# Block transposes inside the out-projection, a later last turn, and one pair of modulation columns as a row on TensorE, in a two-layer encoder

## Chip, cores and metric

One core of a Trainium2 chip. The metric is the device time of one execution in microseconds (us). An execution runs five engines side by side, each with its own stream of instructions in a fixed order: TensorE (PE, matmuls), VectorE (DVE), ScalarE (ACT), GpSimdE (POOL) and SyncE (SP, which here issues the DMA transfers). Products are accumulated in PSUM; operands lie in SBUF.

## The reference

Two layers over 1024 tokens of width 1024, each a mixer and an MLP. Layer A mixes with an mLSTM, layer B with latent attention; what is common to both is this:

```python
def rms_norm(x, g):
    xf = x.astype(jnp.float32)
    y = xf * lax.rsqrt(jnp.mean(xf * xf, axis=-1, keepdims=True) + EPS)
    return (y * g.astype(jnp.float32)).astype(x.dtype)

def modulate(h, shift, scale):
    return h * (1 + scale[:, None, :]) + shift[:, None, :]
...
    c_act = jax.nn.silu(c)
    for layer in range(DEPTH):
        sh1, sc1, g1, sh2, sc2, g2 = jnp.split(c_act @ mod_w[layer] + mod_b[layer], 6, axis=-1)
        h = modulate(rms_norm(x, norm_g[layer, 0]), sh1, sc1)
        if layer < N_A:
            y = mlstm_mixer(h, a_w_in[layer], a_b_gates[layer], a_head_norm[layer], a_w_out[layer])
        else:
            ...
            y = mla_mixer(h, b_w_qa[j], b_q_norm[j], b_w_qb[j], b_w_o[j], k_nope, k_rope, v, cos, sin)
        x = x + g1[:, None, :] * rms_norm(y, norm_g[layer, 1])
        h = modulate(rms_norm(x, norm_g[layer, 2]), sh2, sc2)
        y = sq_relu_mlp(h, ffn_w1[layer], ffn_w2[layer])
        x = x + g2[:, None, :] * rms_norm(y, norm_g[layer, 3])
    return x
```

At the end of the mLSTM mixer stands `(sigmoid(o_pre) * rms_norm(hh)) @ w_out`. All is in fp32.

## The kernel before

**Products.** An fp32 product is made of three passes of a shorter format: each operand is split into a high part (a cast on ACT, tiles `whi`, `hSh`, `hTh`, `aTh`) and a low part (a subtraction on DVE, `wlo`, `hSl`, `hTl`, `aTl`). `mm3` issues high by high (L159), low by high (L160) and high by low (L161). The tiles lie in a few rotating buffers: PSUM tiles of two banks (`mm`) and of one (`sm`). A tile that is asked for again waits until its last reader is done. The order of each engine's instructions is fixed when the program is built, from the order of the code and from a scheduler's estimate of when things are ready; `issue_after` pins the instructions in it behind a given one.

**The start.** The token blocks are normed and then modulated with per-column scale and shift. Blocks 0 to 3 come first: ACT squares them, DVE makes the reciprocal root (`rsqrt`), ACT scales them by it (L945), PE transposes them by columns k (128 of the 1024 each), and ACT applies the column's scale and shift while it reads PSUM (tile `t`, L953) and casts it. The scale and shift (`modcol`) are a product of a vector `cact` with a 1024x2048 part of `mod_w`, which arrives in `slab` tiles, two columns k to a slab, four units of 512 KB each. Column 0 is made by PE from 16 matmuls of one column (L1011). The others are summed on DVE over the rows (`mod_sum`, L998 and L1000: one TENSOR_SCALAR and seven SCALAR_TENSOR_TENSOR) and turned into a column by a matmul with ones (L1008). The first products are the value projections of blocks 0 to 3, one group for each k.

**The mLSTM's end.** `mlstm_chunk` is a generator that makes one chunk of 128 tokens. Its tail takes the denominators (`dd`), squares, a reciprocal root, and the normed chunk `hn`. Behind the last chunk `gate_split` transposes the first chunk's `hn` on PE, multiplies it by the gate (`gt`, L1366, DVE) and splits it: the first operand of the out-projection.

**The mixer's end** (the same code in layers A and B). `out_proj` makes the eight blocks of tokens in the order 0, 2, 4, 6, 1, 3, 5, 7 (counted by n): 48 matmuls of 128x512 for each. Behind each product `mixer_out` issues the residual (L194 square on ACT, reciprocal root, L419 and L420 on DVE; L419 is the last reader of the PSUM tile), its store to DRAM, and `h_norm` (L512 square, root, L515 scale, tile `h`). Pairs of normed blocks are turned: 16 transposes on PE (L199) into four `sm` tiles, each emptied by two modulating ACT instructions (L475, tile `hr`). The MLP multiplies 2x2 block matrices with seven products in place of eight, so it needs the parts A11, A12 (even blocks), A21, A22 (odd blocks) and the sums S1 to S4 of them (`odd_sums`, four DVE operations of 128x1024, L494 to L497), each as high and low (`odd_high`, L456, ACT; `odd_low`, L460, DVE). `h_even` turns two even blocks and splits them, `odd_turn` turns two odd ones; j is 0 for the first half of the tokens and 2 for the second.

**The MLP's start.** `mlp_begin` issues for pairs p = 0 to 7 of weight columns the first and second product, `up(p)`, of 24 matmuls together: the first needs the even blocks, the second too. Between them stand the turns and splits of what the other products need. The weights come from DRAM (`raw`), are cast (`whi`, L525) and subtracted (`wlo`, L527), one pair after the other. The result is read from PSUM by a copy (L711, ACT) and an addition (L704, DVE).

Of the kernel before, what the change touches and what calls it, by code (L numbers as in the profile page):

```python
# [21 lines left out]
P = 128  # L22
# [43 lines left out]
class Trunk:  # L66
# [338 lines left out]
    def out_proj(self, aT, w):  # L405

        ps = self.MM()
        for k in range(KD):
            a = tuple(u[:, k * P : (k + 1) * P] for u in aT)
            for dh in range(2):  # L410
                o = slice(dh * 512, dh * 512 + 512)
                self.mm3(ps[:, o], a, tuple(u[:, o] for u in w[k]), k == 0, k == KD - 1)
        return ps
# [237 lines left out]
    def mlp_begin(self, l, odd):  # L651
# [9 lines left out]
        up(0, 3, 4, 5)  # L661
        self.odd_high(0, "S1", "A22", "S4")
        up(1, 4, 5, 6)
        self.odd_turn(2, [odd.pop(5), odd.pop(7)])
        self.odd_low(0, "S1", "A22", "S4")
        up(2, 5, 6, 7)
        self.odd_sums(2)
# [17 lines left out]
    def up_product(self, p, s):  # L685
# [10 lines left out]
        for k in range(4):  # L696
            a = tuple(u[:, k * P : (k + 1) * P] for u in w)
            b = tuple(u[:, (k % 2) * 512 : (k % 2) * 512 + 512] for u in h[k // 2])
            self.mm3(ps, a, b, k == 0, k == 3)
        self.w_used((0, p), s)  # L700
# [210 lines left out]
    def layer_a(self):  # L911
# [74 lines left out]
        def slab_part(k, i):  # L986

            return slabs[k // 2][i // 2][:, i % 2, :, (k % 2) * P : (k % 2 + 1) * P]

        def mod_sum(k, n):  # L990

            acc = self.U("acc")[:, : 2 * n * P].rearrange("p (s c) -> p s c", s=2)
            o = (k % 2) * P
            for i in range(KD):
                src = slabs[k // 2][i // 2][:, i % 2, :, o : o + n * P]
                c = self.cact[:, i : i + 1]
                if i == 0:
                    V.tensor_scalar(out=acc, in0=src, scalar1=c, scalar2=None, op0=ALU.mult)  # L998
                else:
                    V.scalar_tensor_tensor(out=acc, in0=src, scalar=c, in1=acc, op0=ALU.mult, op1=ALU.add)  # L1000
            for j in range(n):
                sums[k + j] = acc[:, :, j * P : (j + 1) * P]

        def mod_col(k, acc, ps):

            for s in range(2):
                if acc is not None:
                    PE.matmul(ps[:, s : s + 1], acc[:, s], self.ones[:, 0:1], start=True, stop=True)  # L1008
                else:
                    for i in range(KD):  # L1010
                        PE.matmul(ps[:, s : s + 1], slab_part(k, i)[:, s], self.cact[:, i : i + 1], start=i == 0, stop=i == KD - 1)  # L1011
# [5 lines left out]
        def turned(k):  # L1017

            ps = self.MM()
            mod_col(k, sums.pop(k, None), ps[:, 512:])  # L1020
# [16 lines left out]
        with self.tc.issue_after(normed(xs[:4], True)):  # L1037
            mod_sum(1, 1)
            turned(0)
            turned(1)  # L1040
            mod_sum(2, 2)
        w, acc = [], [None] * 4
        for k in range(KD):
# [10 lines left out]
            if k % 2 and k + 1 < KD:  # L1054
                turned(k + 1)
                turned(k + 2)
                if k + 3 < KD:
                    mod_sum(k + 3, 2)
# [5 lines left out]
        finish(late)  # L1064
# [812 lines left out]
```

## Time and profile before

| | |
|---|---|
| median of 3 runs | 2320.07 us (2318.72 to 2323.43) |
| profiled execution, its own time | 2321.05 us |
| its span, first to last instruction | 2319.3 us |
| PE busy | 2212.0 us (95%), 10758 matmuls |
| DVE busy | 1705.0 us (74%) |
| ACT busy | 1028.0 us (44%) |
| POOL busy | 466.4 us (20%) |
| mean granted clock of TensorE | 0.986 |
| out-projection of layer A, B ends | about 496.6, 1644.7 us |

The span is 1.75 us shorter than the execution's own time, which takes in what lies around it. A profile row gives the start of a group of like instructions, the time that the group took, the engine, the line, what is written from what, the shape and how many there were; in brackets stands how long the engine stood idle before it, and what released it. Matmuls overlap: the end of one is modelled and lies behind the start of the next.

### The profile page before, as it was taken

What the parts mean: (1) busy time and instruction counts of PE and PEld (TensorE: products, weight loads), DVE (VectorE), ACT (ScalarE), POOL (GpSimd) and SP (SyncE); (2) the same over time, 40 slices, a digit from 0 to 9 for tenths busy, and PEclk for the clock granted to TensorE, in tenths of its full rate; (3) what the DMA queues carried; (4) which work ended last, traced back from release to release, by engine and by line L of the source; (5) the groups of instructions that cost most, each with busy time, mean ns of one, the idle gap of its engine ahead of it and who ended that gap; (6) DMA issues with size and microseconds to landing.
All of it is one profiled execution on the core that took longest, in us unless ns stands there. A gap on an engine that the chain in (4) does not pass through costs nothing.

```text
span 2319.3 us, 28894 instructions
## 1 busy us (share of the span) xinstructions
PE 2212.0 (95%) x10758; PEld 1846.3 (80%) x10758; DVE 1705.0 (74%) x2510; ACT 1028.0 (44%) x1709; POOL 466.4 (20%) x317
## 2 busy tenths in 40 slices
PE   6999999979999999999999999999799999999998
PEld 5888887868777877777798989988687888777776
DVE  5685687546987767888978676664569877588888
ACT  3511466554444454333244545555634544633322
POOL 0000110003443343331011000000045434333300
PEclk9999999989999999999999999999899999999999
DMA  8476353233774465445422000113347545544452
GB/s 274 134 285 218 125 131 115 80 100 104 252 249 147 150 195 161 130 142 153 131 74 59 12 17 11 46 64 100 91 140 236 191 147 187 175 130 140 150 168 107
DMA packets 300068, 320.17 MB, mean 138 GB/s; under 512 B 16040, under 2 KB 252184, under 8 KB 299928
## 3 DMA queue, kind: packets, MB, share of 16 engines
q1 hardware_dynamic: 299928, 318.33, 43.6%
q8 instruction: 85, 1.39, 0.3%
q14 instruction: 55, 0.45, 0.1%
HBM read 245.85 MB, written 72.43 MB: 137 GB/s over the span
## 4 chain that ended last, share of the span: by engine, by line
PE 66%; DVE 12%; issue 10%; ACT 4%; DMA 4%; POOL 4%; SPq 0%; POOLq 0%; DVEq 0%; ACTq 0%
PE mm L159 12%; PE mm L160 12%; PE mm L161 12%; PE sm L159 8%; PE sm L160 8%; PE sm L161 8%; PE sm L199 3%; DVE wlo L573 2%; DVE y L784 1%; DVE ul L778 1%; DMA modw<-in_mod_w_dram 1%; POOL tt L600 1%; DVE x L704 1%; DMA slab<-in_mod_w_dram 1%; POOL tt L580 1%
## 5 line engine op out<-in xcount | busy, mean ns | idle before, releaser
L159 PE MATMUL mm<-whi,uh 128*128 128x512 f32 x688 | 273.5, 398 | 11.2 <-DVE y L784 10.9
L161 PE MATMUL mm<-whi,ul 128*128 128x512 f32 x688 | 271.2, 395 | 1.2 <-DVE ul L778 1.2
L160 PE MATMUL mm<-wlo,uh 128*128 128x512 f32 x688 | 271.5, 395 | 0.0
L600 POOL TENSOR_TENSOR tt<-raw,tt 128x512 f32<-128x512 f32 x60 | 113.7, 1895 | 624.3 <-DVE wlo L573 624.3
L784 DVE TENSOR_TENSOR y<-y,mm 128x1024 f32<-128x1024 f32 (+1 forms) x161 | 193.5, 1208 | 51.3 <-PE mm L161 51.1
L159 PE MATMUL sm<-hSh,whi 128*128 128x512 f32 x560 | 222.4, 397 | 9.2 <-DVE x L704 9.2
L160 PE MATMUL sm<-hSl,whi 128*128 128x512 f32 x560 | 221.5, 396 | 0.0
L161 PE MATMUL sm<-hSh,wlo 128*128 128x512 f32 x560 | 220.2, 396 | 0.4 <-DVE wlo L573 0.2
L704 DVE TENSOR_TENSOR x<-x,sm 128x512 f32<-128x512 f32 x198 | 132.4, 682 | 60.9 <-PE sm L161 57.0
L778 DVE TENSOR_TENSOR ul<-u,uh 128x896 fp32r<-128x896 f32 (+1 forms) x120 | 151.2, 1290 | 33.5 <-ACT uh L772 25.9
L573 DVE TENSOR_TENSOR wlo<-raw,whi 128x1024 fp32r<-128x1024 f32 x104 | 155.2, 1492 | 19.8 <-ACT whi L569 19.8
L159 PEld LDWEIGHTS mm<-whi,uh 128*128 128x128 f32 x688 | 129.3, 188 | 47.5 <-DVE y L784 15.8
L580 POOL TENSOR_TENSOR tt<-raw,raw 128x512 f32<-128x512 f32 x32 | 59.9, 1871 | 517.9 <-PE sm L161 488.3
L161 PEld LDWEIGHTS mm<-whi,ul 128*128 128x128 f32 x688 | 129.4, 188 | 32.2 <-DVE ul L778 2.1
L160 PEld LDWEIGHTS mm<-wlo,uh 128*128 128x128 f32 x688 | 129.4, 188 | 29.2
L772 ACT CAST uh<-u 128x896 fp32r<-128x896 f32 (+1 forms) x120 | 108.0, 945 | 85.0 <-PE mm L161 66.9
L159 PEld LDWEIGHTS sm<-hSh,whi 128*128 128x128 f32 x560 | 105.6, 189 | 36.5 <-DVE x L704 7.0
L707 ACT ACTIVATE x<-x 128x1024 f32<-128x1024 f32 x64 | 67.8, 1059 | 148.0 <-DVE x L704 147.8
L161 PEld LDWEIGHTS sm<-hSh,wlo 128*128 128x128 f32 x560 | 105.7, 189 | 26.0 <-DVE wlo L573 1.2
L160 PEld LDWEIGHTS sm<-hSl,whi 128*128 128x128 f32 x560 | 105.7, 189 | 24.2
L569 ACT CAST whi<-tt 128x1024 fp32r<-128x1024 f32 x60 | 62.9, 1048 | 139.2 <-issue 62.2
L283 DVE SCALAR_TENSOR_TENSOR acc<-modw,cact,acc 128x1024 f32<-128x1024 f32 x84 | 113.6, 1352 | 12.1 <-DMA modw<-in_kv_mod_w_dram 6.0
(415 smaller groups left out, 5833.4 us busy)
## 6 DMA issues: line engine op xcount, KB each, us to landing
raw<-in_ffn_w_dram SPq DMA_DIRECT2D x144, 512.0 KB
u<-us SPq DMA_DIRECT2D x112, 448.0 KB
us<-x SPq DMA_DIRECT2D x92, 512.0 KB
modw<-in_mod_w_dram SPq DMA_DIRECT2D x80, 512.0 KB
x<-xn SPq DMA_DIRECT2D x24, 512.0 KB
x<-x SPq DMA_DIRECT2D x24, 512.0 KB
x<-in_x_dram SPq DMA_DIRECT2D x16, 512.0 KB
slab<-in_mod_w_dram SPq DMA_DIRECT2D x32, 256.0 KB
```

What stands on the lines that cost most here:

```text
L159: mm(out, a[0], b[0], start=start, stop=False)
L160: mm(out, a[0], b[1], start=False, stop=False)
L161: mm(out, a[1], b[0], start=False, stop=stop)
L199: self.PE.transpose(out[: s.shape[-1], j * P : j * P + s.shape[0]], s, self.ident[: s.shape[0], : s.shape[0]])
L283: self.V.scalar_tensor_tensor(out=acc, in0=t, scalar=self.cact[:, k : k + 1], in1=acc, op0=ALU.mult, op1=ALU.add)
L573: V.tensor_tensor(out=x[1], in0=u, in1=x[0].bitcast(F32), op=ALU.subtract)
L580: G.tensor_tensor(out=t1, in0=b12, in1=b11, op=ALU.subtract)
L600: G.tensor_tensor(out=t1, in0=b21, in1=t2, op=ALU.subtract)
L704: V.tensor_tensor(out=dst, in0=src, in1=ps, op=ALU.add)
L772: S.copy(x[0], u)
L778: V.tensor_tensor(out=x[1], in0=u, in1=x[0].bitcast(F32), op=ALU.subtract)
L784: V.tensor_tensor(out=dst, in0=dst, in1=ps, op=ALU.add)
```

## The change

Three places are changed.

In the start, columns 0 and 1 are summed together on DVE. Columns 2 and 3 are made on PE as a row: eight matmuls with `cact` as weights of one column and 512 columns of the slab moving (`mod_row`); ACT copies the row from PSUM, and matmuls with ones turn it into columns. Columns 4 to 7 stay on DVE. `finish(late)`, some small constants, moves behind the second half's values.

At the mLSTM's end, the generator of a chunk stops once more before its tail, and the last chunk's tail is issued behind the first gated block.

At the mixer's end, the turns of blocks 0 and 2, of 4 and 6, and of 1 and 3 are issued in the midst of the fourth, sixth and eighth product of the out-projection (n = 3, 5, 7), after half of its matmuls, by a function that `out_proj` calls; before they stood behind the products n = 3, 5 and 6. The sums of the first odd pair go with its turn, its splits behind the MLP's pairs 0 and 1. The last turn (blocks 5 and 7) moves from behind pair 1 to behind pair 2, and is pinned there behind the last matmul of pair 2.

```diff
-    def out_proj(self, aT, w):
+    def out_proj(self, aT, w, midway=None):
         ps = self.MM()
         for k in range(KD):
+            if midway and k == KD // 2:
+                midway()
...
         up(0, 3, 4, 5)
+        self.odd_high(0, "S2", "S3")
+        self.odd_low(0, "S2", "S3")
+        up(1, 4, 5, 6)
         self.odd_high(0, "S1", "A22", "S4")
-        up(1, 4, 5, 6)
-        self.odd_turn(2, [odd.pop(5), odd.pop(7)])
         self.odd_low(0, "S1", "A22", "S4")
         up(2, 5, 6, 7)
+        with self.tc.issue_after(self.issued):
+            self.odd_turn(2, [odd.pop(5), odd.pop(7)])
         self.odd_sums(2)
...
+        def mod_row(k):
+
+            ps = self.SM()
+            for i in range(KD):
+                PE.matmul(ps[0:1].rearrange("p (s c) -> p s c", s=2), self.cact[:, i : i + 1], slab_part(k, i), start=i == 0, stop=i == KD - 1)
+            row = self.U("acc")[0:1, : 4 * P]
+            S.copy(row, ps[0:1])
+            for j in range(2):
+                sums[k + j] = row.rearrange("p (s c) -> p s c", s=2)[:, :, j * P : (j + 1) * P]
...
         with self.tc.issue_after(normed(xs[:4], True)):
-            mod_sum(1, 1)
-            turned(0)
-            turned(1)
-            mod_sum(2, 2)
+            mod_sum(0)
+        mod_row(2)
+        turned(0)
+        turned(1)
...
-                if k + 3 < KD:
-                    mod_sum(k + 3, 2)
+            if k in (1, 3):
+                mod_sum(k + 3)
...
-            hn.append(finish(now))
+            if j + 1 < NT:
+                hn.append(finish(now))
+            else:
+                next(now)
...
         pre = deque([self.gate_split(order[0], hn[order[0]], sg)])
+        hn.append(finish(now))
...
-            y = self.out_proj(pre.popleft(), w_out)
+            y = self.out_proj(pre.popleft(), w_out, self.mixer_midway(n))
...
+    def mixer_midway(self, n):
+
+        hs = self.mix[6]
+
+        def even(j):
+            self.h_even(j, [hs.pop(t) for t in (2 * j, 2 * j + 2)])
+
+        def odd():
+            self.odd_turn(0, [hs.pop(1), hs.pop(3)])
+            self.odd_sums(0)
+
+        return {3: lambda: even(0), 5: lambda: even(2), 7: odd}.get(n)
+
     def mixer_out(self, n, y):
...
-        if n in (3, 5):
-            j = n - 3
-            self.h_even(j, [hs.pop(t) for t in (2 * j, 2 * j + 2)])
-        elif n == 6:
-            self.odd_turn(0, [hs.pop(1), hs.pop(3)])
...
-        if n == 6:
-            self.odd_sums(0)
-            self.odd_high(0, "S2", "S3")
-            self.odd_low(0, "S2", "S3")
...
+        yield
         dd, r1, sq = (self.W(s, [P, AH]) for s in ("dd", "r1", "sq"))
```

In the start, ACT's instructions stood in this order before: behind the squares of the four blocks (`h_175` to `h_181`) their scaling, then the first column's `t`.

```order
L940 ACTIVATE h_181,ssqs_174<-x_103 128x1024
L945 ACTIVATE x_97<-x_97,rsy_184 128x1024
L945 ACTIVATE x_99<-x_99,rsy_184 128x1024
L945 ACTIVATE x_101<-x_101,rsy_184 128x1024
L945 ACTIVATE x_103<-x_103,rsy_184 128x1024
L953 ACTIVATE t_233<-mm_210,modcol 128x512
L109 CAST hTh_234<-t_233 128x512
L953 ACTIVATE t_248<-mm_239,modcol 128x512
L109 CAST whi_261<-raw_129 128x1032
```

Now the copy of the row (`sm_210` is the PSUM tile of columns 2 and 3) stands between the squares and the scaling:

```order
L946 ACTIVATE h_181,ssqs_174<-x_103 128x1024
L1014 COPY acc_219<-sm_210 1x512
L951 ACTIVATE x_97<-x_97,rsy_184 128x1024
L951 ACTIVATE x_99<-x_99,rsy_184 128x1024
L951 ACTIVATE x_101<-x_101,rsy_184 128x1024
L951 ACTIVATE x_103<-x_103,rsy_184 128x1024
L959 ACTIVATE t_230<-mm_221,modcol 128x512
```

Added ahead of the four scalings is an instruction that needs the last of the eight row matmuls.

At the mixer's end in layer A, ACT had before, from the scaling of blocks 1 and 3 (`h_4231`, `h_4232`), the eight evacuations of their turn, and among them the square of the product of n=6 (`mm_4252`), which begins its residual:

```order
L515 ACTIVATE h_4231<-xn_4089,rsy_4236 128x1024
L515 ACTIVATE h_4232<-xn_4216,rsy_4236 128x1024
L475 ACTIVATE hr_4301<-sm_4302,modcol 128x256 x2
L475 ACTIVATE hr_4301<-sm_4309,modcol 128x256 x2
L475 ACTIVATE hr_4316<-sm_4317,modcol 128x256 x2
L194 ACTIVATE xn_4333,ssq_4334<-mm_4252 128x1024
L475 ACTIVATE hr_4316<-sm_4324,modcol 128x256 x2
L169 ACTIVATE rst_4338<-ssq_4334,eps 128x1
L512 ACTIVATE h_4348,ssqs_4347<-xn_4333 128x1024
```

Now (the product of n=6 is `mm_4240`, that of n=7 `mm_4323`):

```order
L517 ACTIVATE h_4219<-xn_4077,rsy_4224 128x1024
L517 ACTIVATE h_4220<-xn_4204,rsy_4224 128x1024
L194 ACTIVATE xn_4291,ssq_4292<-mm_4240 128x1024
L169 ACTIVATE rst_4296<-ssq_4292,eps 128x1
L514 ACTIVATE h_4306,ssqs_4305<-xn_4291 128x1024
L527 CAST whi_4318<-raw_4238 128x1024
L477 ACTIVATE hr_4348<-sm_4349,modcol 128x256 x2
L477 ACTIVATE hr_4348<-sm_4356,modcol 128x256 x2
L477 ACTIVATE hr_4363<-sm_4364,modcol 128x256 x2
L169 ACTIVATE rst_4310<-ssqs_4305,eps 128x1
L477 ACTIVATE hr_4363<-sm_4371,modcol 128x256 x2
L517 ACTIVATE h_4306<-xn_4291,rsy_4309 128x1024
```

The square, the root and the next norm of n=6 have moved ahead of the evacuations of the turn.

On PE before, behind the last matmul of the out-projection (`mm_4387`), stood pair 0's first product, four transposes of the block of n=6 (`h_4348`), pair 1's first product, pair 0's second, and twelve transposes, those of the block of n=7 (`h_4451`) among them. Of each product the first row stands, of the transposes one:

```order
L161 MATMUL mm_4387<-whi_3580,aTl_4109 128x512
L159 MATMUL mm_4484<-hSh_3969,whi_4103 128x512
...
L199 MATMUL sm_4571<-ident,h_4348 128x128
...
L159 MATMUL mm_4536<-hSh_3969,whi_4247 128x512
...
L159 MATMUL mm_4484<-hSh_3975,whi_4103 128x512
...
L199 MATMUL sm_4571<-ident,h_4451 128x128
```

Now, behind `mm_4323`, stand pair 0 (`mm_4456`), four matmuls of pair 2 (`sm_4565`, `sm_4579`), pair 1 (`mm_4506`), the rest of pair 2 and of pair 0, and then the transposes of `h_4306` and `h_4423`, the blocks of n=6 and 7:

```order
L161 MATMUL mm_4323<-whi_3568,aTl_4097 128x512
L159 MATMUL mm_4456<-hSh_3933,whi_4091 128x512
...
L159 MATMUL sm_4565<-hSh_3933,whi_4318 128x512
...
L159 MATMUL mm_4506<-hSh_3933,whi_4235 128x512
...
L159 MATMUL mm_4456<-hSh_3939,whi_4091 128x512
...
L199 MATMUL sm_4600<-ident,h_4306 128x128
L199 MATMUL sm_4600<-ident,h_4423 128x128
```

The transposes of both blocks have moved from behind 12 and 36 matmuls of the MLP to behind 60.

## Rows read from the trace of the kernel before

**Rows 1.** The page, its part 1: busy time of each engine.

```profile
span 2319.3 us, 28894 instructions
...
PE 2212.0 (95%) x10758; PEld 1846.3 (80%) x10758; DVE 1705.0 (74%) x2510; ACT 1028.0 (44%) x1709; POOL 466.4 (20%) x317
```

**Rows 2.** What PE waited for, whole span: us in total, times, longest.

```profile
PE sm L199 <- ACT h L515: 15.1, 4, 6.6
...
PE mm L159 <- DVE xn L419: 9.4, 2, 4.7
PE sm L159 <- DVE x L704: 9.2, 8, 3.6
```

**Rows 3.** Timeline of PE, mixer end of layer A: start, time, idle before.

```profile
501.27 0.80 PE L159 MATMUL mm<-hSh,whi 128*128 128x512 f32 x1 [4.68 <-DVE xn L419]
...
505.61 0.40 PE L160 MATMUL mm<-hSl,whi 128*128 128x512 f32 x1
505.84 0.39 PE L161 MATMUL mm<-hSh,wlo 128*128 128x512 f32 x1
512.36 1.12 PE L199 MATMUL sm<-ident,h 128*128 128x128 f32 x4 [6.13 <-ACT h L515]
...
521.76 1.53 PE L199 MATMUL sm<-ident,h 128*128 128x128 f32 x12 [1.58 <-ACT h L515]
...
557.28 0.50 PE L159 MATMUL mm<-hSh,whi 128*128 128x512 f32 x1 [0.22 <-ACT x L711]
```

**Rows 4.** Timeline of PE, mixer end of layer B.

```profile
1649.35 0.79 PE L159 MATMUL mm<-hSh,whi 128*128 128x512 f32 x1 [4.68 <-DVE xn L419]
...
1705.76 0.51 PE L159 MATMUL mm<-hSh,whi 128*128 128x512 f32 x1 [0.22 <-ACT x L711]
```

**Rows 5.** Timeline of ACT, mixer end of layer A.

```profile
494.24 2.84 ACT L475 ACTIVATE hr<-sm,modcol 128x256 f32<-128x256 f32 x6 [5.85 <-PE sm L199]
496.95 1.05 ACT L194 ACTIVATE xn<-mm 128x1024 f32<-128x1024 f32 x1
...
511.16 1.15 ACT L515 ACTIVATE h<-xn,rsy 128x1024 f32<-128x1024 f32 x1 [1.51 <-DVE rsy L177]
```

**Rows 6.** Timeline of DVE, mixer end of layer A.

```profile
499.93 1.28 DVE L419 SCALAR_TENSOR_TENSOR xn<-mm,rsy,row 128x1024 f32<-128x1024 f32 x1
...
502.39 1.22 DVE L494 TENSOR_TENSOR hs<-hr,hr 128x1024 f32<-128x1024 f32 x1
```

**Rows 7.** Timeline of PE at the end of the mLSTM.

```profile
393.95 1.12 PE L199 MATMUL sm<-ident,hn 128*128 128x128 f32 x4 [4.79 <-DVE gt L1366]
```

**Rows 8.** Timeline of DVE at the end of the mLSTM.

```profile
391.13 0.17 DVE L180 TENSOR_SCALAR rsv<-sq 128x4 f32<-128x4 f32 x1 [2.14 <-ACT hn L1352]
...
393.21 0.68 DVE L1366 TENSOR_TENSOR gt<-sm,sg 128x512 f32<-128x512 f32 x1
```

**Rows 9.** Timeline of PE in the start.

```profile
26.85 1.52 PE L159 MATMUL sm<-whi,hTh 128*128 128x344 f32 x4 [2.08 <-ACT whi L109]
...
30.74 0.46 PE L159 MATMUL sm<-whi,hTh 128*128 128x344 f32 x1
31.03 0.33 PE L160 MATMUL sm<-wlo,hTh 128*128 128x344 f32 x1
...
44.72 1.84 PE L1008 MATMUL mm<-ones,acc 128*128 128x1 f32 x8 [3.01 <-DVE acc L1000]
...
56.24 1.02 PE L1008 MATMUL mm<-ones,acc 128*128 128x1 f32 x8 [0.52 <-DVE acc L1000]
```

**Rows 10.** Timeline of ACT in the start.

```profile
12.40 4.26 ACT L945 ACTIVATE x<-x,rsy 128x1024 f32<-128x1024 f32 x4 [2.28 <-DVE rsy L188]
23.75 0.78 ACT L953 ACTIVATE t<-mm,modcol 128x512 f32<-128x512 f32 x1 [7.09 <-PE mm L199]
```

**Rows 11.** Timeline of PE in the last mLSTM chunk: a plain fp32 product.

```profile
382.16 0.60 PE L1335 MATMUL sm<-Cst,nw 128*128 128x258 f32 x2
```

**Rows 12.** Timeline of SP in the start: issue of the second slab.

```profile
11.44 5.49 SPq L983 DMA_DIRECT2D slab<-in_mod_w_dram  x8
```

**Rows 13.** The chain that ended last, in the start: start, us, what.

```profile
15.44 6.38 DMA slab<-in_mod_w_dram
```

More of the change, by code (lines that the diff above doesn't have):

```diff
@@ L699, in up_product @@
             self.mm3(ps, a, b, k == 0, k == 3)
+        self.issued = self.last()
         self.w_used((0, p), s)
@@ L986, in slab_part, with mod_sum @@
         def slab_part(k, i):
[L988 to L993, printed above, removed]
+            return slabs[k // 2][i // 2][:, i % 2]
+        def mod_sum(k):
+            acc = self.U("acc")[:, : 4 * P].rearrange("p (s c) -> p s c", s=2)
             for i in range(KD):
-                src = slabs[k // 2][i // 2][:, i % 2, :, o : o + n * P]
                 c = self.cact[:, i : i + 1]
                 if i == 0:
-                    V.tensor_scalar(out=acc, in0=src, scalar1=c, scalar2=None, op0=ALU.mult)
+                    V.tensor_scalar(out=acc, in0=slab_part(k, i), scalar1=c, scalar2=None, op0=ALU.mult)
                 else:
-                    V.scalar_tensor_tensor(out=acc, in0=src, scalar=c, in1=acc, op0=ALU.mult, op1=ALU.add)
-            for j in range(n):
+                    V.scalar_tensor_tensor(out=acc, in0=slab_part(k, i), scalar=c, in1=acc, op0=ALU.mult, op1=ALU.add)
+            for j in range(2):
                 sums[k + j] = acc[:, :, j * P : (j + 1) * P]
+        def mod_row(k):
[4 more added lines that the diff above has]
+            S.copy(row, ps[0:1])
+            for j in range(2):
+                sums[k + j] = row.rearrange("p (s c) -> p s c", s=2)[:, :, j * P : (j + 1) * P]
         def mod_col(k, acc, ps):
             for s in range(2):
[L1007 to L1011, printed above, removed]
+                PE.matmul(ps[:, s : s + 1], acc[:, s], self.ones[: acc.shape[0], 0:1], start=True, stop=True)
             bias = self.bcols[:, : 2 * KD].rearrange("p (s k) -> p s k", s=2)[:, :, k]
@@ L1019, in turned @@
             ps = self.MM()
-            mod_col(k, sums.pop(k, None), ps[:, 512:])
+            mod_col(k, sums.pop(k), ps[:, 512:])
             self.transposes(ps, [x[:, k * P : (k + 1) * P] for x in xs[:4]])
@@ L1063, in layer_a @@
                 self.mm3(acc[tb][:, :VP], self.hT_tb(hT, tb, k), tuple(u[:, o : o + VP] for u in w[k // 3]), k == 0, k == KD - 1)
-        finish(late)
         w1 = [self.take(("v", 1, g)) for g in range(3)]
@@ L1075, in layer_a @@
                     modulate(k, ps, self.U("t")[:, :512], *hT_part(1, k, slice(0, 512)), k % 2 == 1)
+        finish(late)
         self.ahead, self.early = 3, 3
@@ L1770, in layer_b_out @@
                 pre.append(split(self.ORDER[n + 2]))
-            self.mixer_out(n, self.out_proj(pre.popleft(), w_o))
+            self.mixer_out(n, self.out_proj(pre.popleft(), w_o, self.mixer_midway(n)))
     def run(self):
```

## The prediction

> **What bounds the kernel now.** The page first: PE is busy 2212.0 of 2319.3 us [rows 1], so what can be won without removing PE's work is the 107 us in which it stands, and the stretches in which a stand has left its clock at half rate. Next the table of what PE waits for [rows 2]: 15.1 us for a normed block (ACT h, L515) and 9.4 for a residual (DVE xn, L419), both at the end of the two mixers. Then the timeline at the three places that the change touches.
>
> Mixer end, layer A [rows 3]. The last output product has issued at T = 501.27 − 4.68 = 496.59. PE then waits 4.68 us for the residual of n=6 (it frees the PSUM tile), 6.13 and 1.58 us for the last block's h, 0.22 us for a copy, and begins pair 7's second product at 557.28: T + 60.7. The code issues in between 15 products of 12 matmuls and 16 transposes. At full clock a matmul starts 0.23 us after the one before (505.61, 505.84), and the 12 transposes at 521.76 take 1.53, so the work is 180×0.232 + 1.7 = 43.4 us. The other 17.3 are 12.6 of waits and 4.7 of half clock: from 501.27 to 505.61 ten matmuls start 0.43 apart (1.2 in place of 2.4 GHz), as they do again behind the 6.13. Layer B is its twin [rows 4]: T = 1644.67, pair 7 at 1705.76, 61.1 us.
>
> Why the residual is late: n=6's product was finished at about 483.4 (behind it lie 48 matmuls of n=7, 11.1 us, and 16 transposes, 2.1), but its square on ACT came at 496.95, behind six evacuations of the odd turn, for which ACT idled 5.85 us [rows 5]: PE makes those transposes in the midst of n=7. Then DVE takes 1.2 us for each of four odd sums between n=6's residual and n=7's [rows 6]. The last h comes at 511.16 + 1.15.
>
> Gate [rows 7, 8]: PE waits 4.79 us to 393.95 for gt. DVE idled 2.14 us for ACT's squares until 391.13, then ran the reciprocal root and a wlo; gt starts at 393.21.
>
> Start [rows 9, 10]: the first projection matmul is at 26.85, at half rate until 31.03; the last columns come at 56.24. ACT scales the four x blocks from 12.40 (4.26 us) and later idles 7.09 us until 23.75.
>
> **Mixer end after.** The even and first odd turns go inside out_proj 3, 5 and 7, where PE has product on both sides, so their transposes (1.7 us each) lie on PE as before; what changes is ACT's order: n=6's square now stands in front of the turn of blocks 1 and 3. Its residual is then done some 9 us before T, so the 4.68 is gone. Pair 0's first product starts at T and lasts 2.8; four matmuls of the next tiles, to T + 3.7; then pair 1's waits for the PSUM tile of n=7, freed by n=7's residual. For n=6 that chain took from ACT's 496.95 to the end of L419 at 501.21, 4.3 us; n=7's square comes at T + 0.4 and part of the odd sums stands in front on DVE, so I take T + 5.3: a new wait of 1.6. Then 44 matmuls (10.2 us) to T + 15.5. There stand the first transposes of the last turn; h of block 7 should be ready by T + 13.7 (511.16 + 1.15 is T + 15.7 before, less about 2 as its own residual no longer follows n=6's). So the 6.13 is covered by work that before stood behind it. The second eight transposes need a PSUM bank that ACT must empty: 0.8 us. PE never stands for long, so I expect full clock throughout: pair 7 at T + 43.4 + 2.4, with 0.7 for what I have not seen T + 46.5. Gain 14.2 in A, 14.6 in B; I take 14 and 14.3. Bounds: no new wait and full clock, 17.3 and 17.7; or each of the two waits 1 us longer, 12 each. SP's queue keeps its order but for two stores that move by a place, so the weights of the pairs come as before relative to those stores; they were needed 14 us later, which is the cover I trust least.
>
> **Gate after.** The tail of the last chunk (root, squares, normalisation) is issued behind the first gated block. gt then needs only the transposes (done at 393.95 − 4.79 = 389.2) and DVE's wlo, and that wlo waits for ACT's cast, which now follows the copies of the chunk with no squares between. gt comes about 2.8 us earlier; the tail itself belongs to the last chunk, wanted only at the last product, 90 us on. Gain 2.5 (1.5 to 3).
>
> **Start after.** Removed: 16 PE matmuls of one column, DVE's sum for column 1 and for 2 and 3. Added: DVE's 512-wide sum for columns 0 and 1 (as cheap as the slab's arrival: eight operations, under 1 us each), eight matmuls of 512 columns in fp32 with a one-column weight, a copy of one row. No row shows such a matmul. The nearest is the fp32 128x258 [rows 11]: two records in 0.60 us, of which some 0.17 is a matmul's tail, so 0.43 for 258 columns and 0.85 for 512; 1.71 at half clock. The eight cost 6.8 to 13.7 us on an engine that idles there. But they read the second slab: its eight transfers are issued from 11.44 to 16.9 [rows 12], and the one handed over at 15.44 lands 6.38 later, at 21.8 [rows 13]; with 6 us of lag units of two land from about 17.9 to 22.4. Starting at 17.9 at half clock, with the clock up after 4.2 us as at 26.85, the rows end at R = 17.9 + 4.2 + 5.5×0.85 = 26.8; all at half clock 31.6; only bound by arrival 23.3.
>
> ACT's order decides what that costs: the copy of the row stands in front of the four scalings of x, so these go from 12.40 to R + 0.6. That ACT does not pass a waiting instruction shows in its 7.09 us [rows 10]: the cast of the first weights, which were issued ahead of the second slab [rows 12] and so landed by about 18, stands behind t in the order and PE waited for it until 26.85 [rows 9]. If ACT could pass it, the scalings would stay at 12.40, the start cost nothing and the sum be 5 us lower. The Trainium skill has the rule too (Perfetto Trace Analysis, section Tensor Engine Instruction: of ACT, DVE and GPSIMD it says "strict FIFO"). By that rule the copy holds up the scalings; the trace agrees, with its 7.09. So, by the row: copy and scalings to R + 4.9, transposes, t at R + 5.3, and, as from 23.75 to 26.85, the first projection matmul 3.1 later: R + 8.4 = 35.2, against 26.85. Columns 2 and 3 are there by then, so not all of this lasts. The sum for 4 and 5 on DVE has in its midst a wlo whose cast stands on ACT behind column 3's t, and that behind 22 projection matmuls: R + 8.4 + 6.3 (0.287 each at half rate, the step from 30.74 to 31.03 in rows 9) + 2.8 (transposes, t, cast) + 5.1 (wlo, five sums) = R + 22.6. From there to the columns of 6 and 7 it is as before from 44.72 to 56.24, 11.5: R + 34.1 = 60.9 against 56.24. A loss of 4.7, with 0.3 for casts I have not followed: +5. The late constants, moved behind the second half, return less than 1 us and I leave them out. Bounds +0.5 and +10, from R = 23.3 and 31.6.
>
> **Sum.** −14 − 14.3 − 2.5 + 5 = −25.8 from the profiled execution's 2321.05: 2295.3. That execution is 1.0 above the median of the three, so 2294.3 to 2295.3; I say 2295. By the bounds −37.5 to −15.5: 2284 to 2305.
>
> **The rivals.** (a) *Gain given back in the MLP.* PE reaches the later products 14 us sooner; there it already waits 9.2 us for DVE's sums (L704) [rows 2], 3.6 at once, and weights arrive at their own pace. If half of each layer's gain is eaten: −7.1×2 − 2.5 + 5 = −11.7, 2309. Against: most of these waits are below 1.3 us, so DVE keeps up on average and its work starts sooner too. (b) *The wait replaced.* n=7's residual behind the odd sums (4.9 us more on DVE if all four stand in front), the last h behind an ACT cast whose weights are late: PE then stands 5 us or so at pair 1 or at the last turn, with half clock after it. Gain 7 a layer, again about 2309. (c) *Cheap start:* the rows keep to the arrivals, R = 23.3 and loss 1: 2291. (d) *Slower:* one mechanism, the row matmuls. Everything in the start stands behind R, and each us of it is a us of the start once DVE's slack is gone (R + 34.1 against 56.24). The mixer and gate give 30.8; the kernel is slower when the start loses more, R above 53, which is 4.4 us per row matmul, five times the price by rows 11. At 5 us each: R = 58, loss 36, 2325. Only that no row shows a one-column weight speaks for it. (e) *Nothing moves:* all gains refilled by the DVE and weight chain; 2316 to 2325. The gate's gain alone would speak against it.
>
> **How the numbers follow.** Chances: forecast 0.52; (a) 0.14; (b) 0.14; (c) 0.08; (d) 0.04; (e) 0.08, of which 0.06 within 0.2% and 0.01 on each side. A measurement of this kernel tells 0.2%, 4.6 us, from no change. The forecast, (a), (b) and (c) are faster by more, 0.88, and with 0.01 of (e) 0.89; same 0.06; slower 0.04 + 0.01. The range reaches from the favourable bound to rivals (a) and (b) and a little past them: 2284 to 2311; left out are (d), (e) and the worse ends of (a) and (b), under 2 in 10.
>
> **What would show it.** Right: PE's wait for L419's line is gone behind the last output product, that for h below 2 us, pair 7's second product at T + 46; gt some 2.8 us earlier after the hn transposes; in the start x's scalings behind a one-row copy at about 27, first projection matmul at about 35, last columns at about 61. Wrong: row records far from 0.85 us; a wait over 3 us at pair 1's product or at the last turn's transposes; PE waits for weights (whi) in pairs 4 to 7; waits for L704's line grown by 10 us.

## The result, and the profile after

The changed kernel takes 2294.34 us in the median (2293.41 to 2296.04, 4 runs), against 2321.04 (2318.72 to 2323.43, 4 runs) for the kernel before: a ratio of 0.9886, interval 0.9869 to 0.9903. It is faster, by 26.7 us. Forecast were 2295, 2284 to 2311. The profiled execution took 2293.41.

The page's part 1 of the changed kernel:

```profile
span 2291.6 us, 28854 instructions
...
PE 2203.1 (96%) x10746; PEld 1831.5 (80%) x10746; DVE 1701.0 (74%) x2502; ACT 1028.5 (45%) x1710; POOL 470.8 (21%) x317
```

PE still bounds the kernel [rows 1]. The span fell by 27.7 us and PE's busy time by 8.9, with 12 matmuls fewer: part of the gain is matmuls that no longer run at half clock. Where it came from is read as the distance between the same instruction in both traces (the start of A's last output matmul is 496.19 before and 498.78 after):

| stretch (PE) | before | after | gained | forecast |
|---|---|---|---|---|
| span's start to the transposes of `hn` | 387.19 | 393.76 | −6.6 | −5 |
| from there to A's last output matmul | 109.00 | 105.02 | 4.0 | 2.5 |
| from there to pair 7's second product, A | 61.09 | 47.14 | 13.95 | 14 |
| from there to B's last output matmul | 1086.99 | 1085.62 | 1.4 | 0 |
| from there to pair 7's second product, B | 61.49 | 47.07 | 14.4 | 14.3 |
| from there to the end | | | 0.55 | 0 |

**Mixer end.** PE's waits of the changed kernel from 470 to 560 us, the whole list (what waited, for what: us in total, times, longest):

```profile
PE mm L159 <- DVE xn L421: 0.9, 1, 0.9
PE sm L159 <- DVE x L710: 0.5, 1, 0.5
PE mm L159 <- ACT x L717: 0.2, 1, 0.2
```

Timeline of PE there (start, time; idle before):

```profile
499.01 0.39 PE L159 MATMUL mm<-hSh,whi 128*128 128x512 f32 x1
...
503.82 0.50 PE L159 MATMUL mm<-hSh,whi 128*128 128x512 f32 x1 [0.93 <-DVE xn L421]
504.16 0.39 PE L160 MATMUL mm<-hSl,whi 128*128 128x512 f32 x1
504.39 0.40 PE L161 MATMUL mm<-hSh,wlo 128*128 128x512 f32 x1
...
514.12 1.03 PE L199 MATMUL sm<-ident,h 128*128 128x128 f32 x8
...
545.92 0.50 PE L159 MATMUL mm<-hSh,whi 128*128 128x512 f32 x1 [0.21 <-ACT x L717]
```

Against [rows 3], where 4.68, 6.13 and 1.58 us of waits stood, with half clock behind the first two: one wait of 0.93 is left for the residual, the matmuls behind it start 0.23 apart (full clock), and the transposes wait for nothing. Layer B repeats it [rows 4]:

```profile
1636.57 0.51 PE L159 MATMUL mm<-hSh,whi 128*128 128x512 f32 x1 [0.90 <-DVE xn L421]
...
1678.61 0.50 PE L159 MATMUL mm<-hSh,whi 128*128 128x512 f32 x1 [0.21 <-ACT x L717]
```

Timelines of ACT and then DVE in layer A:

```profile
486.32 1.03 ACT L194 ACTIVATE xn<-mm 128x1024 f32<-128x1024 f32 x1 [0.17 <-PE mm L161]
...
493.09 2.84 ACT L477 ACTIVATE hr<-sm,modcol 128x256 f32<-128x256 f32 x6
...
499.21 1.03 ACT L194 ACTIVATE xn<-mm 128x1024 f32<-128x1024 f32 x1 [1.16 <-PE mm L161]
...
511.42 1.15 ACT L517 ACTIVATE h<-xn,rsy 128x1024 f32<-128x1024 f32 x1
```

```profile
488.52 1.28 DVE L421 SCALAR_TENSOR_TENSOR xn<-mm,rsy,row 128x1024 f32<-128x1024 f32 x1
...
497.05 1.23 DVE L496 TENSOR_TENSOR hs<-hr,hr 128x1024 f32<-128x1024 f32 x1 [0.30 <-ACT hr L477]
...
502.48 1.28 DVE L421 SCALAR_TENSOR_TENSOR xn<-mm,rsy,row 128x1024 f32<-128x1024 f32 x1
```

The square of n=6 (486.32) now stands ahead of the six evacuations, not behind them as in [rows 5], and its residual is done 9.2 us before pair 0 starts. All four odd sums still precede n=7's residual, but they begin 2 us before pair 0 [rows 6 had them later].

**Gate.** PE behind the transposes of `hn`, to the first output product:

```profile
397.64 1.25 PE L199 MATMUL sm<-ident,hn 128*128 128x128 f32 x8 [1.91 <-DVE gt L1385]
398.65 0.48 PE L159 MATMUL mm<-whi,aTh 128*128 128x512 f32 x1
398.96 0.39 PE L160 MATMUL mm<-wlo,aTh 128*128 128x512 f32 x1
```

The wait is 1.91, against 4.79 [rows 7]. Here the output matmuls run at full clock from the first; before, they began at half clock, 0.43 apart (from 394.72 to 399.56, 4.8 us):

```profile
397.00 0.63 PE L159 MATMUL mm<-whi,aTh 128*128 128x512 f32 x1
397.42 0.63 PE L160 MATMUL mm<-wlo,aTh 128*128 128x512 f32 x1
...
399.56 0.45 PE L159 MATMUL mm<-whi,aTh 128*128 128x512 f32 x1
```

A little later the changed kernel has a wait that the kernel before has not, for a low part of the out-projection's weights; ACT now makes the last chunk's squares (398.74 to 400.72) in front of the casts of these weights, which before followed the gated block at once (395.12):

```profile
408.73 0.50 PE L160 MATMUL mm<-wlo,aTh 128*128 128x512 f32 x1 [1.23 <-DVE wlo L110]
```

**Start.** PE, then ACT:

```profile
18.44 8.78 PE L1012 MATMUL sm<-slab,cact 128*1 128x512 f32 x16 [8.29 <-DVE acc L1004]
...
35.75 1.01 PE L1021 MATMUL mm<-ones,acc 1*128 1x1 f32 x4
36.69 1.52 PE L159 MATMUL sm<-whi,hTh 128*128 128x344 f32 x4
...
61.16 1.02 PE L1021 MATMUL mm<-ones,acc 128*128 128x1 f32 x8 [0.66 <-DVE acc L1004]
```

```profile
27.25 0.57 ACT L1014 COPY acc<-sm 1x512 f32<-1x512 f32 x1 [16.93 <-PE sm L1012]
27.74 4.26 ACT L951 ACTIVATE x<-x,rsy 128x1024 f32<-128x1024 f32 x4
32.42 0.78 ACT L959 ACTIVATE t<-mm,modcol 128x512 f32<-128x512 f32 x1 [0.43 <-PE mm L199]
...
34.43 1.04 ACT L109 CAST whi<-raw 128x1032 fp32r<-128x1032 f32 x1
```

The rows end at 27.2, and behind them go copy, scalings and `t`, 15.3 us later than the scalings in [rows 10]. (The releaser named for the rows, DVE's sum, merely ended then; they read the slab and not the sum.)

### The profile page after: what moved, and what is told of

It reads as the page before. It is cut to its first block, busy times and chain, and to the rows that moved or that the text cites. A ratio compares the mean times of both kernels' runs of the same rounds, so it can differ in the third digit from the quotient of the medians.

```text
span 2291.6 us, 28854 instructions
## 1 busy us (share of the span) xinstructions
PE 2203.1 (96%) x10746; PEld 1831.5 (80%) x10746; DVE 1701.0 (74%) x2502; ACT 1028.5 (45%) x1710; POOL 470.8 (21%) x317
## 4 chain that ended last, share of the span: by engine, by line
PE 62%; DVE 12%; issue 11%; ACT 5%; POOL 4%; DMA 4%; SPq 0%; POOLq 0%; DVEq 0%; ACTq 0%
PE mm L159 11%; PE mm L160 11%; PE mm L161 11%; PE sm L159 8%; PE sm L160 8%; PE sm L161 8%; PE sm L199 3%; DVE wlo L575 2%; DVE y L790 1%; DVE ul L784 1%; POOL tt L602 1%; DVE x L710 1%; POOL tt L583 1%; POOL raw L595 1%; POOL tt L582 1%
## 5 line engine op out<-in xcount | busy, mean ns | idle before, releaser
L710 DVE TENSOR_TENSOR x<-x,sm 128x512 f32<-128x512 f32 x198 | 132.4, 682 | 54.9 <-PE sm L161 52.0
L607 ACT CAST w<-tt 128x512 fp32r<-128x512 f32 x60 | 37.2, 619 | 191.9 <-POOL tt L602 188.4
```

Source lines behind the costliest of these rows:

```text
L710: V.tensor_tensor(out=dst, in0=src, in1=ps, op=ALU.add)
```

## The experiments

All are the changed kernel with one thing altered, unless said otherwise; times are medians to be held against its 2294.34, the ratio is to the kernel before.

**start_old.** The start of before, all else as changed (`mod_row` gone, column 0 by 16 matmuls, `mod_sum(1, 1)`, `mod_sum(2, 2)`, late constants last).

> The changed kernel with the start of before (columns 1 to 7 on DVE, column 0 by one-column matmuls, late constants ahead of the first values); gate and mixer ends stay changed. Theory: the new start costs 6.5 us by the two traces (the last mLSTM chunk's transposes stood 6.57 later than before), of which about 1.8 is half clock behind the gates' wait at 125 us and may fall elsewhere. So 2294.3 - 6.5 = 2288, at most 2290; the first projection matmul at 26.9 and the last columns at 56.2 as in [rows 9]. Rival: the start's loss is taken up later by the waits that stand between, and the time stays at 2294.

2288.59 (2286.68 to 2290.07), 0.9857 [0.9843, 0.9872]. The new start costs 5.75.

**copy_behind.** The row's copy pinned behind the scalings (`scaled` is the last of them):

```diff
+        scaled = self.last()
...
-        mod_row(2)
+        with self.tc.issue_after(scaled):
+            mod_row(2)
```

> The changed kernel, but the one-row copy is issued behind the four scalings of x on ACT; the eight row matmuls stay ahead of the transposes of x on PE. Theory (ACT's order holds up the scalings): they go back to about 12.5, and t needs only the end of the rows, the columns 0 and 1 and the transposes on PE: 27.2 + 0.9 + 1.1 = 29.2 in place of 32.4, the first projection matmul about 33.4 in place of 36.7, the time about 2291. Rival (the rows on PE themselves set the start, the scalings are hidden): t stays within 0.5 us of 32.4 and the time at 2294.

2288.41 (2287.08 to 2290.38), 0.9858. ACT:

```profile
13.11 4.26 ACT L951 ACTIVATE x<-x,rsy 128x1024 f32<-128x1024 f32 x4 [2.27 <-DVE rsy L188]
27.55 0.57 ACT L1014 COPY acc<-sm 1x512 f32<-1x512 f32 x1 [10.18 <-PE sm L1012]
29.06 0.78 ACT L959 ACTIVATE t<-mm,modcol 128x512 f32<-128x512 f32 x1 [0.94 <-PE mm L199]
```

The row ends as late as before, yet `t` comes 3.4 us earlier, the first projection matmul at 32.55 (36.69) and the last columns at 56.81, near the 56.24 of the kernel before [rows 9]. The 5.9 us are all of the start's loss, nearly twice the 3.3 that I expected.

**row_later.** The row's matmuls also pinned, behind the transposes of columns 0 and 1.

> The changed kernel, but the eight row matmuls are pinned on PE behind the transposes of columns 0 and 1, so that neither the scalings nor these transposes wait for the rows. Theory: transposes at 19 to 21, rows from 21 to about 29.5 while ACT and DVE make t and the first weights, first projection matmul at about 31 in place of 36.7, and most of it lasts: 5 us, 2289, about where the start of before puts it. Rival: DVE's two sums (columns 4 and 5, then 6 and 7) set the end of the start anyway; then the last columns stay later than 59 us (61.2 in the changed kernel) and the time falls by 2 us at most, 2292.

2288.83 (2288.62 to 2290.18), 0.986. The rows run from 22.93 to 31.98, the copy at 32.02 holds up the cast of the first weights, and the first projection matmul is at 34.04 (31 expected); the last columns at 56.13. Three starts with the scalings early are alike within 0.5 us: the row as such brings nothing, and the copy ahead of the scalings is what cost.

**gate_old.** The old order of the last chunk's tail (the `yield` and the split of `finish(now)` taken out).

> The changed kernel with the last chunk's tail ahead of the first gated block again. Theory by the traces: the wait for gt goes back from 1.9 to 4.8 us and the first output matmuls run at half clock again: 2.6 + 1.3 = 4.0 more, 2298.3. Rival (only the wait counts, as forecast): 2.5 more, 2296.8. Third: the mixer's end takes it up, 2294.

2299.78 (2297.89 to 2302.82), 0.9909: +5.4. PE:

```profile
401.04 1.12 PE L199 MATMUL sm<-ident,hn 128*128 128x128 f32 x4 [4.79 <-DVE gt L1380]
401.81 0.78 PE L159 MATMUL mm<-whi,aTh 128*128 128x512 f32 x1
402.38 0.63 PE L160 MATMUL mm<-wlo,aTh 128*128 128x512 f32 x1
```

The wait of 4.79 is back, and with it matmuls 0.43 apart. It costs more than the wait alone: from the transposes of `hn` to A's last output matmul PE takes 108.91 us (394.28 to 503.19) against 105.02 in the changed kernel. To within 0.2, these 3.9 are 2.9 of the wait and 2.4 of half clock, less the 1.2 of the wait for `wlo`, which stands in the changed order alone. The other 1.5 of the 5.4 lies outside the stretch that was edited.

**mid_old.** The turns where they stood, the last turn as changed:

```diff
-            y = self.out_proj(pre.popleft(), w_out, self.mixer_midway(n))
+            y = self.out_proj(pre.popleft(), w_out)
...
+        if n in (3, 5):
+            j = n - 3
+            self.h_even(j, [hs.pop(t) for t in (2 * j, 2 * j + 2)])
+        elif n == 6:
+            self.odd_turn(0, [hs.pop(1), hs.pop(3)])
...
+        if n == 6:
+            self.odd_sums(0)
```

> The changed kernel with the turns issued where they stood before (behind products 3, 5 and 6, the odd sums behind product 6), the last turn still pinned behind pair 2. On ACT the square of n=6 stands behind six turn evacuations again. Theory (the order on ACT and DVE behind the turn carries most of the gain): pair 0 waits 4.7 us for n=6's residual and pair 1 some 3.6 for n=7's behind the odd sums, with half clock after each: 10 us a layer, 2294 + 20 = 2314. Rival (the later last turn carries it, since it covers the wait for the last block): only the 4.7 with its half clock comes back, 6 a layer, 2306.

2316.11 (2312.5 to 2318.19, 11 runs), 0.9976 [0.9967, 0.9985]: +21.8. PE waits for both residuals, and the half clock returns behind each:

```profile
505.60 0.80 PE L159 MATMUL mm<-hSh,whi 128*128 128x512 f32 x1 [4.69 <-DVE xn L421]
...
514.89 0.50 PE L159 MATMUL mm<-hSh,whi 128*128 128x512 f32 x1 [3.99 <-DVE xn L421]
```

From the last output matmul to pair 7's second product PE takes 56.61 us in A (500.51 to 557.12) and 56.34 in B (1645.03 to 1701.37), against 47.14 and 47.07: 18.7 of the 21.8.

**last_old.** The last turn behind pair 1 and not pinned, the midway turns kept:

```diff
         up(1, 4, 5, 6)
+        self.odd_turn(2, [odd.pop(5), odd.pop(7)])
         ...
         up(2, 5, 6, 7)
-        with self.tc.issue_after(self.issued):
-            self.odd_turn(2, [odd.pop(5), odd.pop(7)])
```

> The changed kernel with the last turn behind pair 1 and not pinned, as before the change; the other turns stay in the midst of the products. Theory: block 7 is ready at T + 13.6 as in the changed kernel's trace, and PE has 36 matmuls and the wait for n=7's residual ahead of its transposes, until about T + 10.7: a wait of 3 us and 2 of half clock, 4 to 5 a layer, 2303. Rival (the midway turns alone suffice, the pin is worth nothing): within 1 us a layer, 2294 to 2296.

2300.09 (2297.58 to 2300.74), 0.9906: +5.8, between the theory's 2303 and the rival's 2296. PE waits at the mixer end of A:

```profile
501.00 0.51 PE L159 MATMUL mm<-hSh,whi 128*128 128x512 f32 x1 [1.40 <-DVE xn L421]
...
504.86 0.50 PE L159 MATMUL mm<-hSh,whi 128*128 128x512 f32 x1 [0.80 <-ACT x L716]
...
509.84 2.82 PE L199 MATMUL sm<-ident,h 128*128 128x128 f32 x12 [1.92 <-ACT h L517]
...
547.07 0.50 PE L159 MATMUL mm<-hSh,whi 128*128 128x512 f32 x1 [0.22 <-ACT x L716]
```

B ends the same way:

```profile
1685.19 0.50 PE L159 MATMUL mm<-hSh,whi 128*128 128x512 f32 x1 [0.21 <-ACT x L716]
```

From the last output matmul (495.98 and 1635.98) to these rows PE takes 51.09 and 49.21 us, against 47.14 and 47.07 for the same matmuls and transposes in the changed kernel: 4.0 in A and 2.1 in B. In both, the waits are some 2.5 us longer; in A 3.4 us at half clock follow the wait for `h`, in B the clock stays full. So the 6.1 at the two mixer ends account for the whole of the 5.8, by the theory's reason; the theory's 4 to 5 a layer is met in A and twice too high in B.

The start of the same instruction in the two traces hides this, because the clock moves it elsewhere. last_old stands 2.8 us ahead when A's mixer end begins (495.98 against 498.78), from the gates on, where its clock stays full and that of the changed kernel falls (its window stands below). Between pair 7 in A and B's last output matmul it loses 3.3 (1.15 behind to 4.43 behind), where the order of instructions is the same in both, most of it at two places, 1376 to 1386 and 1533 to 1536 of the changed kernel's time. Windows of last_old, then of the changed kernel (stretch, length, busy us of PE, PEld, DVE, ACT, POOL; PE clock; DMA share; GB/s):

```profile
120.00:135.00 15.00, 13.36 (x66) 11.16 (x67) 12.74 (x23) 4.19 (x6) 0.00 (x0) 1.00 0.70 240
1500.00:1550.00 50.00, 46.53 (x294) 42.37 (x293) 34.59 (x66) 27.59 (x62) 0.00 (x0) 0.93 0.24 74
```

```profile
1500.00:1550.00 50.00, 46.10 (x292) 40.97 (x291) 32.87 (x64) 27.40 (x61) 0.00 (x0) 1.00 0.23 74
```

No edit is in reach of either stretch.

**no_pin.** The last turn behind pair 2, only the pin taken away (`if True:` for `with self.tc.issue_after(self.issued):`).

> The changed kernel with the last turn in the code where it stands now, behind pair 2, but not pinned behind pair 2's last matmul. The order then puts two transposes of block 6 ahead of pair 1; the rest of the last turn stands where it did. Theory (the place in the code is what counts, the pin only guards it): within 1 us a layer, 2293 to 2296. Rival (an early transpose holds a PSUM bank that pair 1 or 2 wants): 2 us or more a layer, 2298.

2295.5 (2293.83 to 2296.28), 0.9886: +1.2, with overlapping ranges. Two of the transposes slip ahead of pair 1, whose wait is 0.70 then; the stretch from the last output matmul to pair 7's second product is 46.94 and 46.95 us. The pin does nothing that this can measure.

**only_mid.** The kernel before with the midway turns alone.

> The kernel before with one part of the change alone: the turns of blocks 0 to 6 in the midst of the products 3, 5 and 7, with the odd sums there and the first odd pair's splits behind pair 0; the start, the gate and the last turn (behind pair 1, not pinned) as before. If the parts add, the changed kernel's 2294.3 less the start's 5.7, plus the gate's 5.4 and the last turn's 5.8 gives 2299.8, 21.5 below before: the midway turns alone carry about 11 us a layer. Rival (the last turn and the midway turns need each other): 2306 or more.

2297.49 (2296.52 to 2298.32), 0.9897: 24.1 below the kernel before in the same comparison (2321.62). Its stretches from the last output matmul to pair 7's second product are 49.20 (495.72 to 544.92) and 49.97 us (1631.47 to 1681.43), 11.9 and 11.5 less than before. With mid_old's +21.8 this puts most of the mixer's gain on the midway turns, from both sides.

**rows_twice.** The row's eight matmuls issued twice; the second pass starts the sum anew, so that nothing is doubled in the result, contrary to what its expectation says.

```diff
-            for i in range(KD):
+            for i in [*range(KD), *range(KD)]:
                 PE.matmul(ps[0:1].rearrange(
```

> The changed kernel with the eight row matmuls done twice into the same row (it leaves columns 2 and 3 doubled before their bias). The rows then end 6.9 us later, at 34.1. Forecast's step (each us of the rows' end is a us of the start): 2294.3 + 6.9 = 2301. Rival (slack on DVE or in the transfers behind takes part of it): 2297 or less.

2293.11 (2292.05 to 2294.94), 0.988: not slower, though the rows end at 34.8. The program's scheduler, seeing a later row, had put the copy behind the scalings, and column 3's transposes ahead of the projection. Against the changed kernel it tells nothing of the step it was made for. Against copy_behind, which has the same order of copy and scalings, it is 4.7 slower with rows that end 7.4 later. The next run pins the order:

**rows_twice_front.** The same, with the scalings held behind the copy as the changed kernel has them.

> The changed kernel with the eight row matmuls done twice (the second pass starts the sum anew) and, unlike the run rows_twice, with the scalings of x held behind the row's copy on ACT as the changed kernel has them. The rows end at about 34. Forecast's step (with ACT's order as it is, each us of the rows' end is a us of the start): 6.9 later, 2301. Rival (the other slack of the start takes most of it, as in rows_twice): 2297 or less.

2300.34 (2296.34 to 2302.47), 0.9906: +6.0. PE, then ACT:

```profile
19.37 16.80 PE L1012 MATMUL sm<-slab,cact 128*1 128x512 f32 x32 [8.30 <-DMA slab<-in_mod_w_dram]
```

```profile
36.20 0.57 ACT L1014 COPY acc<-sm 1x512 f32<-1x512 f32 x1 [24.93 <-PE sm L1012]
36.69 4.26 ACT L1053 ACTIVATE x<-x,rsy 128x1024 f32<-128x1024 f32 x4
```

The rows end 9.0 us later, the copy comes 9.0 later, the first projection matmul 9.1 (45.78), the last columns 8.8 (70.00): each us of R is a us of the start, as rival (d) had it. Some 3 of them do not reach the total.

**dve_pairs.** No row: columns 2 and 3 as a 512-wide sum on DVE too, the later sums a step earlier.

> The changed kernel with no row on PE: columns 2 and 3 are summed on DVE, 512 wide, right behind (as scheduled: interleaved with) columns 0 and 1, and the sums of 4 to 7 are issued one step earlier. If DVE's idle time from 18.4 to 33.9 in the changed kernel is what the start lacks, columns 0 to 3 are there at about 24 (second slab landed at 22.6), first projection matmul at 28, the last columns at 45 in place of 61 (the last slab lands at about 38), and the time falls by 8 to 2286 or below. Rival (the row frees DVE for something that the start needs): no better than the start of before, 2288.6.

2283.4 (2279.94 to 2285.29), 0.9835: −11. The scheduler had mixed the sums of two slabs, and DVE waited 5.47 us for the second slab ahead of columns 0 and 1, which came at 27.43 only; last columns 51.11, not the 45 that I expected.

**dve_pairs2.** The same with the sums pinned, one behind the other (`placed` is an instruction of column 1's shift and scale, `summed` the last of the sum before):

```diff
-        mod_row(2)
         turned(0)
         turned(1)
+        with self.tc.issue_after(self.placed):
+            mod_sum(2)
...
-            if k in (1, 3):
-                mod_sum(k + 3)
+            if k in (0, 2):
+                with self.tc.issue_after(self.summed):
+                    mod_sum(k + 4)
```

> The changed kernel with no row: columns 2 and 3 summed on DVE behind the columns 0 and 1 (pinned, so that the second slab holds up nothing of the first), 4 and 5 behind those, 6 and 7 last. In dve_pairs the scheduler had interleaved the first two sums, DVE stood 5.5 us for the second slab and columns 0 and 1 came at 27.4. Now they come at about 18.5, the first projection matmul at about 23, columns 2 and 3 at 26, the last columns at 45 (51.1 in dve_pairs). 5 us less than dve_pairs, 2278. Rival (the transfers, which end at 45, set the end of the start): 2282.

2281.37 (2278.78 to 2282.21), 0.9825 [0.981, 0.9839]: 13 us below the changed kernel, the fastest here. PE:

```profile
18.31 1.87 PE L1022 MATMUL mm<-ones,acc 128*128 128x1 f32 x8 [8.34 <-DVE acc L1004]
...
24.27 1.51 PE L159 MATMUL sm<-whi,hTh 128*128 128x344 f32 x4 [2.29 <-ACT whi L109]
...
44.92 1.52 PE L1022 MATMUL mm<-ones,acc 128*128 128x1 f32 x8 [0.50 <-DVE acc L1004]
```

Columns 0 and 1 are there at 18.3, the first projection matmul 12.4 us earlier than with the row, the last columns at 44.9, all within 1.3 us of what was expected; columns 2 and 3 come at 30.9, 5 later than expected. The time is 3 above the 2278 expected and near the rival's 2282: the projection behind the last columns begins at 54.94, 10.6 earlier than in the changed kernel, where the columns come 16.2 earlier. What held it between was not tested.

## Why the prediction was right, point by point

**Mixer ends: mechanism and size right.** 13.95 and 14.4 against 14 and 14.3. The steps held: the residual of n=6 early, a new wait at pair 1 (0.93 at T + 4.8; forecast 1.6 at T + 5.3), the last `h` at T + 13.6 (13.7), the transposes at T + 15.1 (15.5) without a wait, full clock throughout. PE's waits are 1.6 in sum (2.4); the remainder that I put at 0.7 is 46.9 − 43.4 − 1.6 = 1.9. Some 1.1 of it is in the traces: 182 matmuls stand there, not 180 (0.5 us), and the 16 transposes take about 2.3 us, not 1.7. The same error stood in the reading of the kernel before: of the 4.7 put down to half clock, the rows give about 3.5 (1.9 behind the wait of 4.68, 1.6 behind that of 6.13). It falls out of the difference.

What the prediction left open, which of the two edits earns this, four runs answer (us from the last output matmul to pair 7's second product; the work is the same in all):

| kernel | midway turns | last turn | A | B |
|---|---|---|---|---|
| before | old | old | 61.09 | 61.49 |
| mid_old | old | new | 56.61 | 56.34 |
| only_mid | new | old | 49.20 | 49.97 |
| last_old | new | old | 51.09 | 49.21 |
| changed | new | new | 47.14 | 47.07 |

The midway turns earn 9.3 to 12.3 us a layer, the later place of the last turn 2.1 to 4.0 beside them and 4.5 to 5.2 without them: each covers in part what the other covers.

**Gate: two parts of the term were missed.** The step "Gain 2.5" counted the wait alone; it fell by 2.9, as the step said (gt 2.8 earlier). What it left out is the half clock behind the old wait: the same eight transposes and nine matmuls take 5.6 us before (393.95 to 399.56) and 3.2 now (397.64 to 400.83), another 2.4. It also left out the new wait of 1.23 for `wlo`, the price of a tail that now stands in front of the weights' casts: 2.9 + 2.4 − 1.2 is 4.1, against the 4.0 measured. At the mixer ends I had counted half clock from [rows 3], and did not look for it behind [rows 7].

**Start: right up to the last columns, 1.6 more behind them.** R came at 27.2 (26.8): the records follow each other 0.43 apart at full clock, two to a matmul, so 0.86 each (0.85), 0.85 apart until 21.8. Then "R + 8.4" is R + 9.5 for the first projection matmul (36.69). `t` was on time (32.42; R + 5.3 is 32.5), and the weights' cast, behind a second `t` as before, ended at 35.47; but PE still had the transposes and one-row matmuls of columns 2 and 3 in front (to 36.69), which the 3.1 taken from [rows 10] and [rows 9] did not hold. The last columns came at 61.16 (60.9), 4.9 later than before. The rest arose later, most of it at layer A's gates: PE waits 2.7 us there in both kernels, but afterwards the clock stays half for longer. Windows of before and then of after around it, shifted by the 5 us (columns as above):

```profile
115.00:130.00 15.00, 13.54 (x60) 11.74 (x61) 12.59 (x22) 4.01 (x6) 0.00 (x0) 0.89 0.64 225
```

```profile
120.00:135.00 15.00, 13.31 (x54) 11.79 (x55) 12.91 (x23) 4.22 (x6) 0.00 (x0) 0.77 0.58 199
```

At 0.89 and 0.77 of 15 us, 1.8 us of full-rate work is missing after. No step of mine foresaw it, and why the clock stays half there I cannot say. It need not be a price of the new start: last_old has the same start (last columns at 61.12) and full clock in that window (1.00, above). In the medians, start_old puts the whole start at 5.75.

The two errors, 1.5 each and of opposite sign, cancelled by luck. The profiled execution gained 27.7, against a sum of 25.8; the rest is the 1.4 and 0.55 at places that the prediction held at nothing, and that execution lies 0.9 below its median. The 1.4 is again mostly clock: at 1543 the kernel before has 3.4 us at half clock that the changed one has not. The total is better than its parts.

**Rivals.** (a) is not seen: PE's waits for the addition are 9.6 us, 10 times (L710), against 9.2, 8 times [rows 2], and layer A's gain is kept to layer B. (b) is not seen either, although all four odd sums do stand ahead of n=7's residual: they begin while PE still multiplies, and for the most part run while DVE would wait for ACT's square. (c) fails at the 8.8 us that the rows take from 18.44: they did not keep to the arrivals, PE's own time set R. (d) had the dependence right, as rows_twice_front shows, and a price five times too high. (e) is refuted by the mixer ends.

**ACT's order.** With the copy ahead, ACT idles 16.93 us and scales x at 27.74; with the copy behind the scalings it scales at 13.11. That agrees with the Trainium skill's "strict FIFO" for ACT (Perfetto Trace Analysis, section Tensor Engine Instruction).

**Open.** Why last_old and others show another clock in stretches where no instruction moved; and why, with the old last turn, it fell behind a wait of 1.92 in last_old's layer A and stayed full behind 1.68 in its layer B.

## What to carry to other kernels

Look for the short instruction that frees a buffer and stands, on its in-order engine, behind longer work that waits for the same busy producer: moving that work into the midst of earlier products freed 9 to 12 us a layer here without removing any. Price a wait of TensorE with the matmuls behind it, not by itself: at the gate the half clock added 2.4 us to a wait that shrank by 2.9, and at the mixer ends it made some 3.5 of 17.3. Price an edit by the stretch that it changes, taken from one instruction to another in each trace, and not by how far the two traces are apart at its end. Before work is moved to an idle engine, follow its result: the row on TensorE was as cheap as estimated, but its copy stood in front of ACT's scalings (5.9 us), and 13 us lay in leaving the row out and pinning the sums.

## What the runs showed that I had not expected

- A scheduler that sees one cost doubled changes the order of other engines: rows_twice did more PE work in the start and was no slower (2293.11 against 2294.34, ranges that overlap). An experiment on one cost needs the order pinned.
- The granted clock differs between kernels in stretches that no edit touches (between last_old and the changed kernel 1.00 against 0.77 over 15 us at the gates, 2.8 us of time, and 0.93 against 1.00 over 50 us from 1500, 1.8 us); differences of 2 to 3 us between two traces are not evidence without the clock of the stretch.
